# Token-tile tail, norm from PSUM, direct operand sums and waits by tile in a one-core hybrid layer

## The chip, the cores and the metric

The kernel runs on one core of a Trainium2 chip. The core has TensorE (PE) for matmuls, VectorE (DVE), ScalarE (ACT), GpSimd (POOL) and SyncE (SP, which here only issues transfers). The metric is the device time of one execution, in microseconds.

## What is computed

One decoder layer on `x` of 1 x 2048 x 1024 in fp32:

```python
h = rmsnorm(x, pre_mix_norm);  p = h @ w_in
mix = concat(pool_mixer(p), ssd_mixer(p), mlstm_mixer(p)) @ w_out
x = x + rmsnorm(mix, post_mix_norm)
h = rmsnorm(x, pre_ffn_norm)
u = causal_dwconv(h @ w_up, conv_w, conv_b)      # 2 x 2816 columns, 3 taps
g, val = split(u)
f = (gelu(g) * val) @ w_down
x = x + rmsnorm(f, post_ffn_norm)
```

## The kernel before

The 2048 tokens are four blocks `s` of 512 (`TB`), each of four token tiles of 128 (`NCK`). All matmuls are in pairs of a high and a low fp32r part: `mm3` (L124) does three matmuls of 128 x 128 by 128 x 512 for one fp32 product, so every operand passes a split: a cast on ACT for the high part, a subtraction on DVE for the low.

The four mixers run first, one block after the other, and store their output transposed in DRAM. Then, for each block: `load_mix` (L708) loads and splits it into two operand tiles of the T buffers; `out_proj` (L717) multiplies it with `w_out` in two halves of 512 columns, 96 matmuls each, with four token tiles in the four PSUM banks of `psm`, and copies each bank out on ACT; `mid_norm` (L726) does the first norm with the residual add (stored to DRAM as `x2_d`) and the second norm; `to_T` (L751) transposes the result on PE, 32 transposes of 128 x 128 per block, copies it out on ACT and stores it in `hT_d`.

The feed-forward layer works on two pairs of blocks. The up and the down matrix products are each done with seven products of half-sized operands in place of eight. `prep_T` (L773) builds their operand sums from `hT_d` and puts the split parts into T0 to T6; `prep_T_last` (L792) loads the last two. `up` (L849) takes 22 column tiles, each with 7 products of 12 matmuls, then the convolution and gelu on ACT, DVE and POOL. `down_first` (L965) does two of the down products (`product`, L933: eleven steps `kp` of 24 matmuls, eight PSUM banks, one per token tile), `down_rest` (L994) the other five, and `finish` (L978) the last norm and the residual add, token tile by token tile. `finish` is called for the second four tiles of a pair after the last product is complete. `up` of the first pair starts between `out_proj` of block 3 and `to_T` of block 3, which it calls after its first column tile (`after_first`, L1093).

The order on each engine is worked out before the run by a scheduler from the program's dependencies; two calls of `keep_in_program_order` (L730, L758) pin single instructions. Each engine then works through its own list in order, as SP's and POOL's queues do with transfers. Pools `bt` (T2 to T6), `bm` and `be` lie over memory that the mixers or `bt` used before, and a first use waits for the whole pool's earlier users. In the names below, `acc0` and `acc1` hold the rows of even and odd blocks, `psm` banks are `mm`, `pss` banks are `sm`.

Of the kernel before, what the change touches and what calls it, by code (L numbers as in the profile page):

```python
# [8 lines left out]
F32 = mybir.dt.float32  # L9
F32R = mybir.dt.float32r  # L10
# [5 lines left out]
P = 128  # L16
# [45 lines left out]
def kernel(  # L62
# [35 lines left out]
    for nm in ("post_mix", "pre_ffn"):  # L98
        nw[nm] = shared.tile([P, DM], F32, tag=nm, name=nm)
    junk = shared.tile([P, DM], BF16, name="junk")  # L100
# [7 lines left out]
    V.memset(mhalf, -0.5)  # L108

# [40 lines left out]
    with ExitStack() as actx:  # L150
# [18 lines left out]
        def load_x(s, ws=None):  # L169
# [41 lines left out]
            (pool_scale[0].rearrange("(t p) -> t p", p=P), 2),  # L211
        ]
# [11 lines left out]
        V.tensor_copy(out=vcol[:, 66:nrow], in_=pv[:, 66:nrow])  # L224
        pbs = ac.tile([P, 2], F32, name="pbs")
# [48 lines left out]
        for nm, src in (("post_mix", post_mix_norm), ("pre_ffn", pre_ffn_norm)):  # L274
            nc.gpsimd.dma_start(out=nw[nm], in_=src[0].partition_broadcast(P))
# [394 lines left out]
    with ExitStack() as bctx:  # L670
        bm = bctx.enter_context(tc.tile_pool(name="bm", bufs=1))
# [16 lines left out]
        bsh.adopt("cv", [a1[:, 3072:4096]])  # L688

# [13 lines left out]
        def rms_scale(t):  # L703
# [13 lines left out]
        def out_proj(mT):  # L717
            mo = [sh.tile([P, DM], F32, tag="acc", name="mo") for _ in range(NCK)]
            lhs = lambda kt: (mT[kt // 4][:, kt % 4, 0], mT[kt // 4][:, kt % 4, 1])
            for hf in range(2):  # L720
                ps = proj_tm(lhs, w_out, 0, KT, hf)
                for tok in range(NCK):
                    S.copy(out=mo[tok][:, hf * 512:(hf + 1) * 512], in_=ps[tok])
            return mo

        def mid_norm(s, mo):  # L726

            ss = sb.tile([P, 2 * NCK], F32, tag="ss4", name="ss4", bufs=1)[:, :NCK]
            for tok in range(NCK):
                i = S.activation(out=junk, in_=mo[tok], func=AF.Square, accum_out=ss[:, tok:tok + 1])  # L730
                if s == 1 and tok == 0:
                    tc.keep_in_program_order(i)
            rs1 = rstd_from(ss, DM, [P, NCK], sb, "n4", 1)
            prev = None
            for tok in range(NCK + 1):
                if tok < NCK:
                    t = mo[tok]
                    r = s * TB + tok * P
                    xt = sh.tile([P, DM], F32, tag="xt", name="xt")
                    nc.sync.dma_start(out=xt, in_=x2d[r:r + P])  # L740
                    V.scalar_tensor_tensor(out=t, in0=t, scalar=rs1[:, tok:tok + 1], in1=nw["post_mix"],
                                           op0=ALU.mult, op1=ALU.mult)
                    V.tensor_tensor(out=t, in0=t, in1=xt, op=ALU.add)
                    nc.sync.dma_start(out=x2_d[s][tok * P:(tok + 1) * P], in_=t)
                    rs = rms_scale(t)
                if prev:
                    V.scalar_tensor_tensor(out=prev[0], in0=prev[0], scalar=prev[1][:, 0:1], in1=nw["pre_ffn"],
                                           op0=ALU.mult, op1=ALU.mult)
                prev = (t, rs)
# [21 lines left out]
        TI = {"T2": 2, "B11": 3, "T1": 4, "T3": 0, "B21": 1, "T4": 5, "B22": 6}  # L771

        def prep_T(sb_, Tt):  # L773

            for kt in range(4):
                l1, l2 = Lm[:, 0:1024], Lm[:, 1024:2048]
                nc.sync.dma_start(out=l1, in_=hT_d[sb_][kt * P:(kt + 1) * P])
                nc.sync.dma_start(out=l2, in_=hT_d[sb_][(kt + 4) * P:(kt + 5) * P])
                a_, b_, c_, d_ = l1[:, :512], l1[:, 512:], l2[:, :512], l2[:, 512:]
                put = lambda n, x: split(x, Tt[TI[n]][:, kt, 0], Tt[TI[n]][:, kt, 1])  # L780
                put("B11", a_)
                V.tensor_tensor(out=a_, in0=b_, in1=a_, op=ALU.subtract)
                put("T1", a_)
                V.tensor_tensor(out=b_, in0=d_, in1=b_, op=ALU.subtract)
                put("T3", b_)
                put("B21", c_)
                V.tensor_tensor(out=a_, in0=d_, in1=a_, op=ALU.subtract)
                put("T2", a_)
                V.tensor_tensor(out=c_, in0=c_, in1=a_, op=ALU.subtract)
                nc.gpsimd.dma_start(out=T4_d[sb_][kt * P:(kt + 1) * P], in_=c_)  # L790

        def prep_T_last(sb_, Tt):  # L792
            for n, src in (("T4", T4_d[sb_]), ("B22", hT_d[sb_][512:1024, 512:1024])):
                t = Tt[TI[n]]
                nc.sync.dma_start(out=t[:, :, 1].bitcast(F32), in_=src.rearrange("(k p) l -> p k l", p=P))
                for h in range(2):
                    d = t[:, 2 * h:2 * h + 2]
                    S.copy(out=d[:, :, 0], in_=d[:, :, 1].bitcast(F32))
                    V.tensor_tensor(out=d[:, :, 1], in0=d[:, :, 1].bitcast(F32), in1=d[:, :, 0].bitcast(F32),  # L799
                                    op=ALU.subtract)  # L800
# [333 lines left out]
```

## Time and profile before

| what | us |
|---|---|
| runs (3), median | 2282.2 |
| lowest and highest run | 2279.72, 2283.53 |
| the profiled execution | 2281.67 |
| its span in the trace | 2280.0 |
| PE busy | 2163.8 |
| DVE busy | 1667.6 |
| ACT busy | 1008.4 |
| POOL busy | 540.0 |

Busy times are shares of one span and overlap. Matmuls are pipelined, so that a matmul's own record is longer than the distance to the next. A granted clock of 1.00 in a window is TensorE's full 2.4 GHz, and 0.50 is its lower level, 1.2 GHz.

### The profile page before, as it was taken

To read this page: it belongs to the slowest core of one execution; us is meant where nothing else is said; L and a number is where in the kernel's file an instruction comes from. 1 tells how busy PE (TensorE), PEld (TensorE's weight loads), DVE (VectorE), ACT (ScalarE), POOL (GpSimd) and SP (SyncE) were. 2 spreads that over 40 slices of the span, in tenths; PEclk is the share of its full clock that TensorE was granted. 3 is DMA by queue.
4 is the path that set the end of the run, shared out by engine and by line. 5 is a ranking of instruction groups with operands and counts; after the bars stand their busy time and mean duration, and the time that the engine had idled before them with its cause. 6 is when DMAs were issued, how large, how long until landed. Compare 5 with 4: busy or idle time off the path is not lost.

```text
span 2280.0 us, 27273 instructions
## 1 busy us (share of the span) xinstructions
PE 2163.8 (95%) x9773; PEld 1752.0 (77%) x9773; DVE 1667.6 (73%) x2374; ACT 1008.4 (44%) x1517; POOL 540.0 (24%) x779
## 2 busy tenths in 40 slices
PE   7999999999997996699999999999999999999994
PEld 5887887878886885478888887788888887788883
DVE  5888888888776576678888777447888788654854
ACT  4454364364353565354444444344444444322432
POOL 3222233222222123555555531000101010000101
PEclk9999999999998998799999999999999999999997
DMA  6444353352352777634444446555655556753753
GB/s 215 121 134 128 105 184 91 115 170 87 108 157 74 246 254 255 215 120 139 148 138 134 135 130 227 170 191 164 209 172 190 195 191 231 286 176 110 232 193 120
DMA packets 223785, 379.66 MB, mean 167 GB/s; under 512 B 15062, under 2 KB 122866, under 8 KB 223649
## 3 DMA queue, kind: packets, MB, share of 16 engines
q1 hardware_dynamic: 192352, 272.67, 37.5%
q0 software_dynamic: 28992, 96.86, 12.0%
q10 hardware_dynamic: 2304, 8.39, 1.1%
q8 instruction: 76, 1.25, 0.2%
q14 instruction: 61, 0.49, 0.1%
HBM read 274.48 MB, written 103.38 MB: 166 GB/s over the span
## 4 chain that ended last, share of the span: by engine, by line
PE 87%; DMA 5%; DVE 3%; ACT 2%; issue 2%; POOL 1%; SPq 0%; DVEq 0%; ACTq 0%; POOLq 0%
PE mm L126 18%; PE mm L127 18%; PE mm L128 18%; PE sm L126 8%; PE sm L128 8%; PE sm L127 8%; PE sm L490 1%; DMA wraw<-in_w_in_dram 1%; PE sm L537 1%; DMA Lm<-hT 1%; DMA T<-Lm 1%; DMA out_dram<-xt 1%; PE sm L493 1%; PE sm L500 1%; PE sm L542 1%
## 5 line engine op out<-in xcount | busy, mean ns | idle before, releaser
L126 PE MATMUL mm<-T,wsp 128*128 128x512 f32 x1152 | 459.7, 400 | 9.9 <-ACT T L182 4.1
L127 PE MATMUL mm<-T,wsp 128*128 128x512 f32 x1152 | 455.6, 396 | 0.0
L128 PE MATMUL mm<-T,wsp 128*128 128x512 f32 x1152 | 453.3, 397 | 0.0
L126 PE MATMUL mm<-wsp,T 128*128 128x512 f32 x748 | 297.6, 402 | 16.6 <-ACT wsp L768 8.5
L127 PE MATMUL mm<-wsp,T 128*128 128x512 f32 x748 | 295.7, 395 | 0.0
L128 PE MATMUL mm<-wsp,T 128*128 128x512 f32 x748 | 292.3, 394 | 0.0
L863 DVE SCALAR_TENSOR_TENSOR acc<-acc,fcol,acc 128x1024 f32<-128x1024 f32 x176 | 235.1, 1336 | 44.7 <-ACT acc L860 40.3
L126 PEld LDWEIGHTS mm<-T,wsp 128*128 128x128 f32 x1152 | 217.6, 189 | 60.5 <-issue 5.5
L127 PEld LDWEIGHTS mm<-T,wsp 128*128 128x128 f32 x1152 | 217.7, 189 | 48.9 <-issue 1.0
L128 PEld LDWEIGHTS mm<-T,wsp 128*128 128x128 f32 x1152 | 217.6, 189 | 49.0 <-issue 0.5
L126 PE MATMUL sm<-T,wsp 128*128 128x512 f32 x528 | 210.6, 399 | 8.7 <-ACT wsp L768 8.0
L128 PE MATMUL sm<-T,wsp 128*128 128x512 f32 x528 | 209.5, 398 | 2.7 <-DVE wsp L769 2.7
L127 PE MATMUL sm<-T,wsp 128*128 128x512 f32 x528 | 209.9, 397 | 0.9 <-DVE T L799 0.9
L118 DVE TENSOR_TENSOR wsp<-wraw,wsp 128x1024 fp32r<-128x1024 f32 x120 | 147.7, 1232 | 78.8 <-ACT wsp L117 78.3
L117 ACT CAST wsp<-wraw 128x1024 fp32r<-128x1024 f32 x120 | 125.9, 1050 | 158.1 <-PE mm L128 79.0
L126 PEld LDWEIGHTS mm<-wsp,T 128*128 128x128 f32 x748 | 141.7, 190 | 49.2 <-ACT wsp L768 9.0
L127 PEld LDWEIGHTS mm<-wsp,T 128*128 128x128 f32 x748 | 141.5, 189 | 30.5 <-issue 0.5
L128 PEld LDWEIGHTS mm<-wsp,T 128*128 128x128 f32 x748 | 140.7, 188 | 30.7 <-DVE T L715 0.2
L768 ACT CAST wsp<-xt 128x512 fp32r<-128x512 f32 (+1 forms) x98 | 80.6, 826 | 144.3 <-PE sm L127 94.8
L769 DVE TENSOR_TENSOR T<-T 128x1024 fp32r<-128x1024 f32 x59 | 72.1, 1223 | 91.6 <-ACT T L768 83.1
L860 ACT ACTIVATE acc<-acc,fcol 128x1024 f32<-128x1024 f32 x88 | 109.9, 1249 | 48.8 <-DVE acc L921 47.8
L768 ACT CAST T<-T 128x1024 fp32r<-128x1024 f32 x59 | 62.1, 1053 | 147.9 <-DMA T<-aop 138.1
(355 smaller groups left out, 3959.7 us busy)
## 6 DMA issues: line engine op xcount, KB each, us to landing
wraw<-in_w_in_dram SPq DMA_DIRECT2D x88, 512.0 KB, 3.7
T<-aop SPq DMA_DIRECT2D x59, 512.0 KB, 3.7
aop<-acc POOLq DMA_DIRECT2D x44, 512.0 KB, 3.1
upS<-Lm POOLq DMA_DIRECT2D x66, 256.0 KB, 3.4
wraw<-in_w_out_dram SPq DMA_DIRECT2D x32, 512.0 KB, 4.2
wraw<-in_ffn_w_down_dram SPq DMA_DIRECT2D x28, 512.0 KB, 4.3
xt<-upS SPq DMA_DIRECT2D x53, 256.0 KB, 4.1
xt<-in_ffn_w_up_dram SPq DMA_DIRECT2D x26, 512.0 KB, 4.5
```

Of the source, the lines that this page charges most:

```text
L117: S.copy(out=sp[:, 0], in_=raw)
L118: V.tensor_tensor(out=sp[:, 1], in0=raw, in1=sp.bitcast(F32)[:, 0], op=ALU.subtract)
L126: T.matmul(out=acc, lhsT=lw[0], rhs=lx[0], start=first, stop=False, skip_group_check=goes_on)
L127: T.matmul(out=acc, lhsT=lw[0], rhs=lx[1], start=False, stop=False, skip_group_check=goes_on)
L128: T.matmul(out=acc, lhsT=lw[1], rhs=lx[0], start=False, stop=last, skip_group_check=goes_on)
L490: T.matmul(out=py[:, h], lhsT=m[:, h], rhs=xd[:, h], start=True, stop=True)
L493: T.matmul(out=po[:, g * 4:g * 4 + 4], lhsT=ck(ccm[g], c), rhs=st[:, g * 4:g * 4 + 4], start=True, stop=True)
L500: T.matmul(out=pst[:, g * 4:g * 4 + 4], lhsT=bt[:, g], rhs=dx[:, g * 4:g * 4 + 4], start=True, stop=True)
L768: S.copy(out=hi, in_=src)
L769: V.tensor_tensor(out=lo, in0=src, in1=hi.bitcast(F32), op=ALU.subtract)
L860: S.activation(out=c, in_=u[:, 2:], func=AF.Identity, scale=fcol[:, 88 + t:89 + t], bias=fcol[:, 132 + t:133 + t])
L863: V.scalar_tensor_tensor(out=c, in0=u[:, k:k + 2 * TB], scalar=fcol[:, k * NU + t:k * NU + t + 1], in1=c, op0=ALU.mult, op1=ALU.add)
```

## The change

1. `product` gets `tail`: with `tail=6`, in the last product only, the steps `kp` 6 to 10 are held back and done token tile by token tile (15 matmuls each), and each token tile's `finish` follows at once. Residual rows are loaded into eight buffers during the product (five slices of `b12m`, three `xt`); the square sum and the `post_ffn` multiply of the right half are done ahead (`weigh`).
2. `out_proj` takes the square sums on ACT and the multiply with `post_mix` on DVE straight from PSUM. `mid_norm` then needs one multiply-add per token tile; the second norm's scale is an ACT copy, and `pre_ffn` is applied in the copy after the transposes (`preT`, one column per k tile). Transposes go by k tile over four token tiles (`turn`, `normed`).
3. Operand sums of the first pair take block 1 directly from the rows that the transposed copy leaves in SBUF; only block 0's half is loaded back from `hT_d`. `prep(0)` stands before `out_proj` of block 2. The T buffers are given out anew: block 1 uses T2 and T3, blocks 2 and 3 both T5 and T6.
4. Pools `bt`, `bm` and `be` wait by tile (`reuse_waits="tile"`); the pins are gone. `down_first` copies through eight buffers of 512 columns instead of whole rows; `spare` takes the place of the `pre_ffn` buffer.

```diff
+        bt = btx.enter_context(tc.tile_pool(name="bt", bufs=1, reuse_waits="tile"))
+        bm = bctx.enter_context(tc.tile_pool(name="bm", bufs=1, side="right", reuse_waits="tile"))
...
         def out_proj(mT):
...
                 for tok in range(NCK):
-                    S.copy(out=mo[tok][:, hf * 512:(hf + 1) * 512], in_=ps[tok])
-            return mo
+                    S.activation(out=junk, in_=ps[tok], func=AF.Square, accum_out=ss[:, hf, tok:tok + 1])
+                    V.tensor_tensor(out=mo[tok][:, c], in0=ps[tok], in1=nw["post_mix"][:, c], op=ALU.mult)
+            return mo, ss
...
+        def mid_norm(s, mo, ss):
+            V.tensor_tensor(out=ss[:, 0], in0=ss[:, 0], in1=ss[:, 1], op=ALU.add)
+            rs1 = rstd_from(ss[:, 0], DM, [P, NCK], sb, "n4", 1)
...
+                V.scalar_tensor_tensor(out=t, in0=t, scalar=rs1[:, tok:tok + 1], in1=xt,
+                                       op0=ALU.mult, op1=ALU.add)
+                nc.sync.dma_start(out=x2_d[s][tok * P:(tok + 1) * P], in_=t)
+                rs = rms_scale(t, xt)
+                S.activation(out=t, in_=t, func=AF.Copy, scale=rs[:, 0:1])
...
+        def turn(s, kt):
+            ps = pss.tile([P, NCK, P], F32, tag="sm", name="ps_tr")
             for tok in range(NCK):
...
+                T.transpose(out=ps[:, tok], in_=cols(s, kt)[:, tok], identity=ident)
+            return ps
...
+        def normed(s, kt):
+            d = cols(s, kt)
+            S.activation(out=d, in_=turn(s, kt), func=AF.Copy, scale=preT[:, kt:kt + 1])
+            c = (s % 2) * TB
+            nc.gpsimd.dma_start(out=r4(hT_d[s // 2][kt * P:(kt + 1) * P, c:c + TB]), in_=d)
+            return d
...
-        def prep_T(sb_, Tt):
+        def prep(sb_):
             for kt in range(4):
...
+                b11, b21 = load_h(sb_, 0, kt), load_h(sb_, 0, kt + 4)
+                if sb_ == 0:
+                    b12, b22 = normed(1, kt), normed(1, kt + 4)
...
-        def product(au, ai, wload, ps, new, also=None):
+        def product(au, ai, wload, ps, new, also=None, tail=NKP):
...
+                    if kp >= tail:
+                        late.append((kp, ua, w, i))
+                        continue
...
+            if late:
+                for t in range(NT):
+                    for kp, ua, w, i in late:
+                        mm(kp, t, ua, w, i)
+                    also(kp, t)
...
+        def finish(tile_, left, right, xt, ss):
+            square_sum(left, ss[:, 0:1])
             V.tensor_tensor(out=ss[:, 0:1], in0=ss[:, 0:1], in1=ss[:, 1:2], op=ALU.add)
+            V.tensor_tensor(out=left, in0=left, in1=nw["post_ffn"][:, h0], op=ALU.mult)
             rs = rstd_from(ss[:, 0:1], DM, [P, 1], sb, "n")
+            for c, t in ((h1, right), (h0, left)):
+                V.scalar_tensor_tensor(out=xt[:, c], in0=t, scalar=rs[:, 0:1], in1=xt[:, c],
+                                       op0=ALU.mult, op1=ALU.add)
...
-            product("au6", 6, w_T4, ps, False)
+            product("au6", 6, w_T4, ps, False, finish_last, 6)
...
+        mo0 = block(0, T_mem)
+        load_mix(1, Tt[2:4])
+        mid_norm(0, *mo0)
+        mo1 = out_proj(Tt[2:4])
+        load_mix(2, Tt[5:7])
+        for kt in range(4):
+            put("B11", kt, normed(0, kt))
+        for kt in range(4):
+            put("B21", kt, normed(0, kt + 4))
...
+        mid_norm(1, *mo1)
+        prep(0)
+        mo2 = out_proj(Tt[5:7])
+        load_mix(3, Tt[5:7])
+        mid_norm(2, *mo2)
+        to_T(2)
+        mo3 = out_proj(Tt[5:7])
+        prep_last(0)
+        mid_norm(3, *mo3)
```

The order on VectorE at the end of the last mixer, before (`bd`, `hn`, `h`, `den` are the mixer's, `mt` its output, `n4v` the norm's scale):

```order
L587 TENSOR_TENSOR mt_1_1639<-sm_274,vcol 128x256
L741 SCALAR_TENSOR_TENSOR acc_195<-acc_195,n4v_5723,post_mix 128x1024 x4
L574 RECIPROCAL den_1572<-den_1572 128x4
L562 SCALAR_TENSOR_TENSOR bd<-bd,ar_1855,sm_455 64x65 x2
L547 TENSOR_TENSOR hn_1557<-sm_274,ar_1855 128x260
L562 SCALAR_TENSOR_TENSOR bd<-bd,ar_1855,sm_455 64x65 x2
L577 TENSOR_TENSOR h_0_1576<-h_0_1576,den_1572 128x256
L548 TENSOR_TENSOR hn_1557<-hn_1557,sm_224 128x260
```

And with the change, from the same `mt` row on:

```order
L589 TENSOR_TENSOR mt_1_1641<-sm_276,vcol 128x256
L575 TENSOR_TENSOR den_1574<-den_1574,ar_1857 128x4
L576 RECIPROCAL den_1574<-den_1574 128x4
L579 TENSOR_TENSOR h_0_1578<-h_0_1578,den_1574 128x256
L580 TENSOR_TENSOR hn_1523<-h_0_1578 128x4x64
L549 TENSOR_TENSOR hn_1559<-sm_276,ar_1857 128x260
L582 TENSOR_REDUCE mss_1582<-hn_1523 128x4
L550 TENSOR_TENSOR hn_1559<-hn_1559,sm_225 128x260
```

The four rows of `mid_norm` of block 0 that stood ahead of the RECIPROCAL are gone from there. The order on TensorE after the last matmul of `out_proj` of block 3, before (`acc_195` holds block 2's rows, `acc_196` block 3's; `x4` counts equal neighbours):

```order
L758 MATMUL sm_363<-ident,acc_195 128x128 x4
L758 MATMUL sm_455<-ident,acc_195 128x128 x4
L126 MATMUL mm_367<-T_5465,wsp_230 128x512
L758 MATMUL sm_224<-ident,acc_195 128x128 x4
L127 MATMUL mm_367<-T_5465,wsp_230 128x512
L128 MATMUL mm_367<-T_5465,wsp_230 128x512
L758 MATMUL sm_224<-ident,acc_196 128x128 x8
L126 MATMUL mm_367<-T_5465,wsp_230 128x512
L127 MATMUL mm_367<-T_5465,wsp_230 128x512
```

And with the change, at block 3's first transposes:

```order
L129 MATMUL mm_368<-T_5462,wsp_248 128x512
L127 MATMUL mm_368<-T_5462,wsp_248 128x512
L128 MATMUL mm_368<-T_5462,wsp_248 128x512
L129 MATMUL mm_368<-T_5462,wsp_248 128x512
L757 MATMUL sm_457<-ident,acc_196 128x128
L757 MATMUL sm_225<-ident,acc_196 128x128
L127 MATMUL sm_276<-T_5465,wsp_231 128x512
L128 MATMUL sm_276<-T_5465,wsp_231 128x512
L129 MATMUL sm_276<-T_5465,wsp_231 128x512
```

Before, block 2's last transposes and block 3's first stand among the first nine matmuls of `up`; with the change 72 matmuls of `up` stand ahead of block 3's first transpose, and none of block 2's is left there. The end of VectorE's list, before (`nv` is the last norm's scale):

```order
L989 SCALAR_TENSOR_TENSOR acc_195<-acc_195,nv_5732,post_mix 128x512
L989 SCALAR_TENSOR_TENSOR acc_196<-acc_196,nv_5732,post_mix 128x512
L989 SCALAR_TENSOR_TENSOR acc_195<-acc_195,nv_5741,post_mix 128x512
L989 SCALAR_TENSOR_TENSOR acc_196<-acc_196,nv_5741,post_mix 128x512
L991 TENSOR_TENSOR xt_250<-acc_195,xt_250 128x512
L991 TENSOR_TENSOR xt_250<-acc_196,xt_250 128x512
L991 TENSOR_TENSOR xt_233<-acc_195,xt_233 128x512
L991 TENSOR_TENSOR xt_233<-acc_196,xt_233 128x512
L991 TENSOR_TENSOR xt_239<-acc_195,xt_239 128x512
L991 TENSOR_TENSOR xt_239<-acc_196,xt_239 128x512
```

And with the change (`ssf` holds square sums, `sm` the last PSUM bank of the product):

```order
L1024 TENSOR_TENSOR ssf<-ssf 128x1
L1025 TENSOR_TENSOR acc_195<-acc_195,post_mix 128x512
L133 TENSOR_SCALAR nv_5738<-ssf 128x1
L1109 TENSOR_TENSOR acc_195<-acc_195,sm_225 128x512
L1028 SCALAR_TENSOR_TENSOR xt_240<-acc_196,nv_5738,xt_240 128x512
L1028 SCALAR_TENSOR_TENSOR xt_240<-acc_195,nv_5738,xt_240 128x512
L1024 TENSOR_TENSOR ssf<-ssf 128x1
L1025 TENSOR_TENSOR acc_195<-acc_195,post_mix 128x512
L133 TENSOR_SCALAR nv_5747<-ssf 128x1
L1028 SCALAR_TENSOR_TENSOR xt_251<-acc_196,nv_5747,xt_251 128x512
L1028 SCALAR_TENSOR_TENSOR xt_251<-acc_195,nv_5747,xt_251 128x512
```

Before, the scale, multiply and add of several token tiles follow the product; with the change each token tile has its own short run, and no separate add is left.

## Rows read from the trace of the kernel before

**Rows 1.** The page: span, and busy time, share and instructions by engine.

```profile
span 2280.0 us, 27273 instructions
...
PE 2163.8 (95%) x9773; PEld 1752.0 (77%) x9773; DVE 1667.6 (73%) x2374; ACT 1008.4 (44%) x1517; POOL 540.0 (24%) x779
```

**Rows 2.** Windows: us, busy time by engine, granted clock, DMA share, GB/s.

```profile
900.00:1000.00 100.00, 66.94 (x265) 50.82 (x265) 64.89 (x69) 37.88 (x59) 51.78 (x61) 0.80 0.55 183
1100.00:1200.00 100.00, 100.00 (x432) 80.82 (x432) 79.64 (x89) 47.57 (x67) 52.16 (x69) 1.00 0.42 137
2200.00:2280.00 80.00, 47.44 (x207) 38.49 (x205) 36.08 (x64) 18.17 (x39) 6.39 (x8) 0.82 0.32 111
```

**Rows 3.** Windows, finer, the same columns.

```profile
721.00:745.00 24.00, 11.55 (x42) 9.12 (x42) 17.97 (x42) 3.32 (x4) 7.22 (x10) 0.51 0.19 54
840.00:884.00 44.00, 44.00 (x200) 35.56 (x199) 30.88 (x39) 22.32 (x38) 13.43 (x14) 1.00 0.79 275
884.00:938.00 54.00, 18.56 (x69) 12.46 (x68) 37.61 (x45) 26.89 (x49) 25.09 (x31) 0.61 0.74 246
938.00:1010.00 72.00, 63.49 (x265) 49.65 (x264) 45.07 (x47) 30.62 (x45) 37.07 (x46) 0.94 0.43 140
```

**Rows 4.** Timeline of TensorE: start, us, line, tiles, count, [idle before and releaser].

```profile
734.20 0.69 PE L585 MATMUL sm<-ident,h 128*128 128x128 f32 x2 [6.74 <-DVE h L582]
...
741.29 0.80 PE L126 MATMUL mm<-wsp,T 128*128 128x512 f32 x1 [4.33 <-ACT T L714]
...
890.80 1.14 PE L758 MATMUL sm<-ident,acc 128*128 128x128 f32 x8 [2.91 <-ACT acc L762]
914.64 1.09 PE L758 MATMUL sm<-ident,acc 128*128 128x128 f32 x4 [20.38 <-ACT junk L705]
...
934.78 0.79 PE L126 MATMUL sm<-T,wsp 128*128 128x512 f32 x1 [7.05 <-ACT wsp L768]
...
1943.18 1.22 PE L126 MATMUL mm<-wsp,T 128*128 128x512 f32 x2 [8.52 <-ACT wsp L768]
```

**Rows 5.** Timeline of TensorE: its last matmul.

```profile
2247.05 0.39 PE L128 MATMUL sm<-wsp,T 128*128 128x512 f32 x1
```

**Rows 6.** Chain that ended last, at its end: start us, us, what.

```profile
2259.01 4.28 DMA xt<-x
...
2264.83 0.15 DVE nv L132
2264.99 5.20 DMA out_dram<-xt
...
2270.20 4.33 DMA xt<-x
...
2274.62 0.69 DVE xt L991
```

**Rows 7.** Groups of instructions after 2247 us: busy us, mean ns, idle before.

```profile
L989 DVE SCALAR_TENSOR_TENSOR acc<-acc,nv,post_mix 128x512 f32<-128x512 f32 x16 | 11.2, 745 | 1.2 <-POOL nv L133 1.2
...
L985 ACT ACTIVATE junk<-acc 128x512 bf16<-128x512 f32 x12 | 7.6, 632 | 5.9 <-DVE ss L986 4.5 <-DVE nv L132 1.0
L133 POOL TENSOR_TENSOR nv<-nv,mhalf 128x1 f32<-128x1 f32 x7 | 5.8, 847 | 13.2 <-DVE ss L986 11.1 <-DVE nv L132 2.1
L985 ACT ACTIVATION_READ_ACCUMULATOR junk<-acc 128x1 f32 x12 | 2.3, 188 | 0.0
L1051 DVE TENSOR_TENSOR acc<-acc,sm 128x512 f32<-128x512 f32 x2 | 1.4, 680 | 0.0
```

**Rows 8.** Timeline of VectorE, end of the last mixer.

```profile
724.01 4.86 DVE L741 SCALAR_TENSOR_TENSOR acc<-acc,n4v,post_mix 128x1024 f32<-128x1024 f32 x4
```

**Rows 9.** Chain that ended last, at the turn to down_rest.

```profile
1938.38 2.48 DVE acc L863 x2
1940.86 1.15 DVE t1m L1007
1942.08 1.06 ACT wsp L768
```

More of the change, by code (lines that the diff above doesn't have):

```diff
@@ L97 @@
     nw = {}
-    for nm in ("post_mix", "pre_ffn"):
-        nw[nm] = shared.tile([P, DM], F32, tag=nm, name=nm)
-    junk = shared.tile([P, DM], BF16, name="junk")
+    nw["post_mix"] = shared.tile([P, DM], F32, name="post_mix")
+    spare = shared.tile([P, DM], F32, name="spare")
+    junk = shared.tile([P, 512], BF16, name="junk")
     sh.adopt("acc", [m[:, i * DM:(i + 1) * DM] for m in acc_mem for i in range(4)])
@@ L272 @@
                 V.memset(icnt[r:r + 64, g // 2, t:t + 1], 1.0 / (t + 1))
[L274 to L275 removed]
+        nc.gpsimd.dma_start(out=nw["post_mix"], in_=post_mix_norm[0].partition_broadcast(P))
         st = ac.tile([P, 8, 64], F32, name="st")
@@ L721, in out_proj @@
                 ps = proj_tm(lhs, w_out, 0, KT, hf)
+                c = slice(hf * 512, (hf + 1) * 512)
                 for tok in range(NCK):
-                    S.copy(out=mo[tok][:, hf * 512:(hf + 1) * 512], in_=ps[tok])
-            return mo
-        def mid_norm(s, mo):
-            ss = sb.tile([P, 2 * NCK], F32, tag="ss4", name="ss4", bufs=1)[:, :NCK]
-            for tok in range(NCK):
[L730 to L749, printed above, removed]
@@ L767, in split, with to_T @@
+        def to_T(s):
+            for kt in range(KT):
+                normed(s, kt)
         def split(src, hi, lo):
@@ L792, in prep_T_last @@
-        def prep_T_last(sb_, Tt):
-            for n, src in (("T4", T4_d[sb_]), ("B22", hT_d[sb_][512:1024, 512:1024])):
-                t = Tt[TI[n]]
[L795 to L800, printed above, removed]
+        TI = {"T2": 0, "B11": 1, "T1": 2, "T3": 3, "B21": 4, "T4": 5, "B22": 6}
@@ L931, with mm @@
         NT = 2 * NCK
-        def product(au, ai, wload, ps, new, also=None):
+        def product(au, ai, wload, ps, new, also=None, tail=NKP):
+            def mm(kp, t, ua, w, i):
+                ts_ = slice(t * P, (t + 1) * P)
+                mm3(ps[t], (ua[:, 0, ts_], ua[:, 1, ts_]), (w[:, 0, i], w[:, 1, i]),
+                    new and kp == 0, kp == NKP - 1, not new)
+            late = []
             for u in range((NKP + 1) // 2):
@@ L965, in down_first @@
         def down_first(between):
-            N = [sh.tile([P, DM], F32, tag="acc", name="n11") for _ in range(NT)]
             ps = banks()
@@ L970, in down_first @@
             for t in range(NT):
-                S.copy(out=N[t][:, h0], in_=ps[t])
+                o = bsh.tile([P, 512], F32, tag="st", name="st")
+                S.copy(out=o, in_=ps[t])
+                nc.sync.dma_start(out=c1_d[t][:, h0], in_=o)
             between()
@@ L1024, in w_T4, with weigh, load_e1 @@
                 return diff(r_, r_, t1(u, n))
-            for t in range(NT):
-                nc.sync.dma_start(out=c21[t], in_=c1_d[t][:, h0])
+            ss = bm.tile([P, 2 * NT, 2], F32, name="ssf")
+            def weigh(tile_, right):
+                square_sum(right, ss[:, tile_, 1:2])
+                V.tensor_tensor(out=right, in0=right, in1=nw["post_ffn"][:, h1], op=ALU.mult)
+            def load_e1(kp):
+                if kp < NT:
+                    nc.sync.dma_start(out=c21[kp], in_=c1_d[kp][:, h0])
             ps = banks()
-            product("au6", 2, w_T1, ps, True)
+            product("au6", 2, w_T1, ps, True, load_e1)
             for t in range(NT):
```

154 lines of the change are left out of this document (76 added, 78 removed).

## The prediction

> **What bounds it now.** The page's busy table comes first: TensorE is busy 2163.8 of 2280.0 us [rows 1], and only what it loses in gaps or at half clock can be won. The windows by 100 us say where: a full window has 432 matmul records, one per 0.2325 us to the finer spacing of the timeline, but 900 to 1000 has 265 at clock 0.80, and the last 80 us have 47.44 us of work [rows 2]. Finer windows show that 884 to 938 holds 69 PE records in 54 us at clock 0.61, while 840 to 884 is full, 44.00 us at clock 1.00, with the DMA engines busy 0.79; 721 to 745 runs at 0.51 [rows 3]. PE's timeline names what it waited for: 6.74 us for the mixer's `h` on DVE, 4.33 for the first operand cast of block 1, 20.38 for the square of mid_norm(3) on ACT ahead of block 3's first transpose, 7.05 for an up weight, 8.52 at the turn to the last products [rows 4]. So the limit is TensorE, except in three places where short chains over ACT, DVE and POOL have no matmuls beside them: 721 to 745, 884 to 1010, and the end. PE's last matmul starts at 2247.05 [rows 5], ending near 2247.4, 32.6 us before the span ends.
>
> The sum is made against the profiled execution, 2281.67 us (1.7 more than its span); the median of the runs is 2282.2, so the same difference gives 0.5 us more there. Measurements of this kernel can tell about 0.2%, 4.6 us.
>
> **Part 1, the stretch from out_proj(1) to the first up products.** From 884 to 1010 us TensorE executed 69 + 265 = 334 instructions [rows 3]: 64 transposes (blocks 2 and 3) and 270 up matmuls. Without gaps and at full clock, 270 x 0.2325 = 62.8 and 64 x 0.14 (eight in 1.14 us [rows 4]) = 9.0, 71.8 of 126 us: 54.2 lost. The order of the change puts block 2's transposes among out_proj(3)'s matmuls and block 3's behind 72 up matmuls instead of 9, so 72 x 0.2325 = 16.7 us cover mid_norm(3). That does not hide it all. The bare chain of mid_norm(3) is: last bank square 0.63 + 0.19 and multiply 0.68, sum and scale 0.15 each, power 0.85 [rows 6, 7]; four multiply-adds of 1024, 4.9 by the four L741 [rows 8]; for the last token tile a square (twice the 0.63), 0.15, 0.85, and a scaled copy, costed like the square: together 11 us. Transposes by column need all four token tiles, so this whole chain counts. About ten casts and splits of weights and operands stand between its links on ACT and DVE, at 0.6 to 0.7 us each for those of 512; that makes about 18 to 22 us, against 16.7. I take a wait of 3 and as much again for half clock behind it: 6 us. For out_proj(2) and (3) I take 3 more: blocks 2 and 3 now use the same T5 and T6, whose casts wait for out_proj(2) to let go of each; and banks are held longer. **Bounds** for all that stays: 2 us (only the overlap's ends) and 22 (the old 20.38 in a new place, partly covered). Taken: 9, nearer to the small end, since row 840 to 884 shows the same two engines keeping up beside full PE.
>
> Bank evacuation: an ACT copy becomes square (0.82) then DVE multiply (0.68) [rows 7], 1.5 us. Block halves use the same four banks; between a bank's last matmul of one half and its first of the next lie 3 x 6 matmuls, 4.2 us. Cover 2.7 us: price nothing, as long as DVE's queue is not later than that. What is removed: mid_norm's separate adds and multiplies by pre_ffn (off PE's path except above) and half of prep(0)'s loads, 8 of 256 KB on SP instead of 8 of 512 KB. The transposed stores stay 32 on POOL's queue. T4 and B22 come by eight loads of 256 KB on SP in place of two of 1 MB, ahead of up weights. These beside the shorter loads I cost at nothing; their cover is out_proj(3), and gone it would be one landing, inside the 22.
>
> The mixer's end: T2's casts no longer wait for the whole pool, so the 4.33 goes. The four L741, 4.86 us ahead of the mixer's last RECIPROCAL on DVE [rows 8], now stand behind its last output; in their place four PSUM multiplies (4 x 0.68 = 2.7) come earlier, while PE still has work. Gain between 4.86 - 2.7 = 2.1 and 4.86, taken 3.0; late next is the mixer's own chain. Part 1: 54.2 + 4.3 + 3.0 - 9 = **52.5 saved**.
>
> **Part 2, the end.** Before, residual rows and stores of eight token tiles go through three `xt` buffers: store, load (4.28), add, store (5.20), load (4.33), add, in turn [rows 6]. The change loads all eight rows during the product (on SP, ahead of later weight loads), weighs the right half in advance, and does the last five of the product's eleven k steps token tile by token tile: 15 matmuls each, 3.49 us, against DVE's 0.68 + 0.68 + 2 x 0.75 + 2 x 0.15 = 3.2 [rows 6, 7]. DVE keeps up. After the last matmul: add 0.68; two multiply-adds of the tile before, 1.49 (the last square, 0.82, lies beside them); 0.15; multiply 0.68; 0.15; power 0.85; two multiply-adds 1.49: 5.5, with handoffs 5.8. Store and program end: the last add of before ends near 2274.62 + 1.29 (as a pair takes) = 2275.9, 4.1 before the end. Sum 9.9 instead of 32.6: **22.7 saved**; bounds 20 (a store of 5.20 and a late scale) to 24.3.
>
> **Part 3, the turn to down_rest.** Its chain is two conv steps (2.48), the first weight difference (1.15), its cast (1.06) [rows 9]; waits by tile let the b12m load start some matmuls earlier, but in DVE's new order three conv steps still precede the difference, on the last up bank. Saved 1; bounds 4 and -3. The turn to down_first keeps its order: 0.
>
> **Part 4, the start.** `spare`'s first load of 512 KB now stands seventh on SP's queue, amid the first input loads: at 275 GB/s [rows 3] it holds the engines 1.9 us. Bounds 0 and 1.9; taken 1 lost. Sum: 2281.7 - 52.5 - 22.7 - 1 + 1 = **2206**. With every bound at its end it is 2194 or 2227.
>
> **Rivals.** *The wait moves, not goes* (0.13): column transposes wait for four token tiles, the chain is late by its old 20.38, and an up weight behind it on ACT by its 7.05 [rows 4]. For it: each engine works its rows in the written order, and DVE was busy 37.61 of 54 us in 884 to 938 [rows 3]. Against: 63 more matmuls stand ahead. 2206 + 27 = 2233.
>
> *PE loses its clock in the out projections* (0.03, slower). Place: the halves of out_proj(1) to (3). If DVE's multiply of a bank is over 2.7 us late half after half, PE waits a little at each group, and as in 721 to 745 the granted clock is 0.51, the 1.2 GHz level [rows 3]. 576 matmuls at 0.465 instead of 0.2325 cost 134: 2340. It is slower than before once more than 75 / 0.2325 = 323 matmuls run so. Against: 840 to 884 cycles the same banks at 1.00. The Trainium skill has such a case (TensorE: Matmul & The Clock Gate, A second HAM failure mode: psum-queue depth-cycling): matmul groups going round PSUM banks with short idle moments between them made the clock swing. By that rule the time is this rival's 2340; the trace disagrees so far, with 1.00 in that window, and no run yet shows the two-engine evacuation.
>
> *The change does not do what it says in one part* (0.02): tile waits that still cover whole pools, or DVE so late that the end stays long: parts 2 and 1 each lose most. About 2282, no change.
>
> **Chances.** Forecast 0.82, of which its own bounds are 2194 to 2227; rivals 0.13, 0.03, 0.02. Range 2192 to 2236, to take in the first rival. Faster by over 0.2%: 0.82 + 0.13 less a hundredth for an unseen mishap, 0.94; within 0.2%: 0.02; slower 0.04.
>
> **What would show it.** Right: first transpose of block 3 after some 72 up matmuls, with a gap of a few us instead of 20.38; clock near 1 in the 100 us after out_proj(3); no 4.33 wait at out_proj(1); the L1028 multiply-adds last on DVE and under 11 us from last matmul to end; the 8.52 still 7 or more. Wrong: a gap above 10 us in front of a transpose or of T5's cast, clock 0.5 inside out_proj, PE waiting between token tiles at the end, or up weights landing late behind prep loads.

## The result, and the profile after

The changed kernel takes 2206.9 us (median of 4 runs, 2202.3 to 2209.2) against 2282.9: the ratio is 0.9666, with a 95% interval of 0.9647 to 0.9686. The forecast was 2206, so the total was met almost exactly; the parts were not, as the runs below show. The profiled execution took 2209.2 us, with a span of 2207.5, which is 72.5 less than the span before. The medians are 75.9 apart. Of the 3.4 us more, 2.3 come from that execution being the slowest of its four, and the rest from the profiled execution of before lying 1.2 under its median. Below, times of the runs are set against 2207.2 us, the mean of the two medians of the changed kernel (this one, and 2207.5 when it ran once more as e11).

The top of the page and finer windows of the changed kernel, the latter answering to [rows 3]:

```profile
span 2207.5 us, 27392 instructions
...
PE 2159.4 (98%) x9773; PEld 1749.0 (79%) x9773; DVE 1662.2 (75%) x2387; ACT 1011.8 (46%) x1541; POOL 547.7 (25%) x779
```

```profile
840.00:884.00 44.00, 44.00 (x207) 35.85 (x206) 26.33 (x38) 26.70 (x45) 9.98 (x13) 1.00 0.78 269
884.00:938.00 54.00, 45.81 (x194) 34.72 (x194) 36.56 (x42) 31.17 (x54) 34.90 (x43) 0.94 0.77 246
938.00:1010.00 72.00, 70.19 (x301) 55.98 (x300) 62.82 (x66) 35.48 (x50) 43.53 (x53) 1.00 0.44 144
```

The window 884 to 938 now holds 194 instructions instead of 69, at clock 0.94 instead of 0.61. Window 840 to 884 stays full at 1.00, with banks now emptied by ACT and DVE one after the other. TensorE's timeline has what is left of the waits of [rows 4]:

```profile
729.70 0.69 PE L587 MATMUL sm<-ident,h 128*128 128x128 f32 x2 [3.34 <-DVE h L584]
733.51 0.69 PE L587 MATMUL sm<-ident,h 128*128 128x128 f32 x2 [3.12 <-DVE h L584]
...
837.33 0.50 PE L127 MATMUL mm<-wsp,T 128*128 128x512 f32 x1 [2.32 <-DVE acc L731]
...
889.70 0.50 PE L127 MATMUL mm<-T,wsp 128*128 128x512 f32 x1 [1.62 <-DVE acc L731]
908.29 0.50 PE L127 MATMUL sm<-T,wsp 128*128 128x512 f32 x1 [1.60 <-DVE acc L936]
913.92 0.66 PE L757 MATMUL sm<-ident,acc 128*128 128x128 f32 x4 [1.24 <-ACT acc L747]
916.10 0.79 PE L127 MATMUL mm<-T,wsp 128*128 128x512 f32 x1 [1.53 <-ACT wsp L776]
...
1893.99 2.08 PE L127 MATMUL mm<-wsp,T 128*128 128x512 f32 x4 [6.70 <-ACT wsp L776]
```

No wait is over 2.4 us between 740 and 1010; the wait for block 3's norm is 1.24 where it was 20.38, and 4.33 at the start of out_proj(1) is gone. Two of block 3's transposes stand behind 72 up matmuls, as forecast; 14 follow behind 84 and 16 behind 96. At the end, TensorE's last matmul and VectorE's last rows:

```profile
2198.33 0.40 PE L129 MATMUL sm<-wsp,T 128*128 128x512 f32 x1
```

```profile
2198.77 0.69 DVE L1109 TENSOR_TENSOR acc<-acc,sm 128x512 f32<-128x512 f32 x1 [0.74 <-PE sm L129]
2199.37 1.41 DVE L1028 SCALAR_TENSOR_TENSOR xt<-acc,nv,xt 128x512 f32<-128x512 f32 x2
2200.70 0.15 DVE L1024 TENSOR_TENSOR ssf<-ssf 128x1 f32<-128x1 f32 x1
2200.77 0.68 DVE L1025 TENSOR_TENSOR acc<-acc,post_mix 128x512 f32<-128x512 f32 x1
2201.37 0.14 DVE L133 TENSOR_SCALAR nv<-ssf 128x1 f32<-128x1 f32 x1
2202.18 1.41 DVE L1028 SCALAR_TENSOR_TENSOR xt<-acc,nv,xt 128x512 f32<-128x512 f32 x2 [0.66 <-POOL nv L134]
```

VectorE waits 0.74 for each token tile's last matmul, so it keeps up; 8.8 us lie between the last matmul's end and the end of the span, 32.6 before.

**Where the 72.5 us came from.** All kernels here execute the same 8424 `mm3` matmuls, so the start of the n-th one can be compared between traces. Times of stretches in us, each the difference of two such starts (the last row: end of the span less the last start and 0.4):

| matmuls | what | before | after | after, again |
|---|---|---|---|---|
| 0 to 500 | start, first mixer | 151.2 | 147.4 | 147.5 |
| 500 to 2200 | mixers | 525.2 | 525.4 | 527.4 |
| 2200 to 2304 | end of the last mixer | 57.0 | 53.1 | 52.3 |
| 2304 to 3150 | the middle: out_proj(1) to the first 270 up matmuls | 269.2 | 233.7 | 233.2 |
| 3150 to 4710 | rest of the first up | 361.8 | 361.9 | 361.9 |
| 4710 to 5000 | turn to down_first | 73.5 | 68.7 | 69.9 |
| 5000 to 7000 | second up | 464.2 | 464.3 | 464.4 |
| 7000 to 7110 | turn to down_rest | 35.9 | 34.2 | 34.3 |
| 7110 to 8423 | last five products | 301.2 | 301.6 | 302.4 |
| end | after the last matmul | 32.6 | 8.8 | 8.8 |

The end gives 23.8, the middle 35.5, the mixer's end 3.9, the start 3.8, the two turns 6.5; the other rows are 0.1 to 0.4 longer.

### The profile page after: what moved, and what is told of

Its sections match the earlier page's. It is cut to its first block, busy times and chain, and to the rows that moved or that the text cites. A ratio compares the mean times of both kernels' runs of the same rounds, so it can differ in the third digit from the quotient of the medians.

```text
span 2207.5 us, 27392 instructions
## 1 busy us (share of the span) xinstructions
PE 2159.4 (98%) x9773; PEld 1749.0 (79%) x9773; DVE 1662.2 (75%) x2387; ACT 1011.8 (46%) x1541; POOL 547.7 (25%) x779
## 3 DMA queue, kind: packets, MB, share of 16 engines
q10 hardware_dynamic: 2304, 8.39, 1.2%
## 4 chain that ended last, share of the span: by engine, by line
PE 89%; DMA 3%; DVE 3%; issue 2%; ACT 1%; POOL 1%; SPq 0%; DVEq 0%; POOLq 0%; ACTq 0%
PE mm L127 19%; PE mm L129 19%; PE mm L128 19%; PE sm L127 8%; PE sm L128 8%; PE sm L129 8%; PE sm L539 1%; PE sm L492 1%; DMA wraw<-in_w_in_dram 1%; PE sm L544 1%; PE sm L502 1%; DMA xt<-mixT 1%; PE sm L495 1%; DMA T<-aop 0%; PE sm L547 0%
## 5 line engine op out<-in xcount | busy, mean ns | idle before, releaser
L777 DVE TENSOR_TENSOR T<-T 128x1024 fp32r<-128x1024 f32 (+1 forms) x75 | 84.6, 1132 | 97.6 <-ACT T L776 97.3
L875 POOL COPY acc<-fhalo 128x2 f32<-128x2 f32 x88 | 43.6, 496 | 410.0 <-DVE acc L882 330.2
L776 ACT CAST T<-T 128x1024 fp32r<-128x1024 f32 (+1 forms) x75 | 71.7, 960 | 145.2 <-DMA T<-aop 129.5
```

The costliest lines, as they stand in the source:

```text
L776: S.copy(out=hi, in_=src)
L777: V.tensor_tensor(out=lo, in0=src, in1=hi.bitcast(F32), op=ALU.subtract)
L875: G.tensor_copy(out=u[:, 0:2], in_=fhalo[:, t])
```

## The experiments

Labels e1 to e12; each time is a median of 4 runs or more, and the ratios with their intervals are to the kernel before.

**e1: the kernel before, with all of block 3's transposes pinned.** This edit alone:

```diff
-                        if s == 3 and tok == hf == j == 0:
+                        if s == 3:
```

> The kernel before, with one edit: all 32 transposes of block 3 are pinned behind everything that stands ahead of them in the program on TensorE, so that some 87 up matmuls (20 us) come first instead of 9. Nothing else of the change. Theory 1 (the big gap was a matter of cover: where the transposes stand): the 20.38 us wait and the 2.75 behind it vanish, the wait for an up weight stays at about 7, and the time falls by 20 to 30 us, to 2253 to 2263. Theory 2 (the chain of mid_norm(3) itself, with its separate multiplies and adds, is what was too long, so work from PSUM is what helps): the wait only moves behind the up matmuls or to the up weights, and less than 10 us is gained, 2273 to 2283.

2280.6 us, ratio 0.9991 (0.9982 to 1.0001): no gain. Its timeline of TensorE:

```profile
893.89 1.60 PE L758 MATMUL sm<-ident,acc 128*128 128x128 f32 x8 [2.92 <-ACT acc L762]
923.57 0.80 PE L126 MATMUL mm<-T,wsp 128*128 128x512 f32 x1 [25.95 <-ACT T L768]
...
937.29 0.80 PE L126 MATMUL sm<-T,wsp 128*128 128x512 f32 x1 [5.61 <-ACT wsp L768]
```

The wait for block 3's norm is gone (its first transpose stands behind 96 up matmuls in this trace), and 25.95 us stand in its place, for the cast of an operand tile T: an up operand that prep_T(0) had not finished. So the 20.38 of [rows 4] was only the first in TensorE's list of two chains that ended close together. The second can be seen in the chain of waits of the kernel before, where prep_T(0) goes through one buffer, `Lm`, and DRAM:

```profile
909.57 6.80 DMA T<-Lm
916.39 8.27 DMA Lm<-hT
```

A buffer is stored, 6.80, and only then loaded again, 8.27, for the next of four steps. Its loads ran from 852 to 925 us, after out_proj(2). Neither theory named this chain; of the two, the second's time holds.

**e2: the kernel before, with the new end alone.** The edit is part 1 of the change in `product`, `finish`, `finish_first` and `finish_last`; the square sums lie in a spent buffer.

```diff
...
-            product("au6", 6, w_T4, ps, False)
-            for t in range(NT):
-                V.tensor_tensor(out=c21[t], in0=c21[t], in1=ps[t], op=ALU.add)
-                finish(NT + t, c21[t], c22[t])
+            product("au6", 6, w_T4, ps, False, finish_last, 6)
```

> The kernel before, with part 1 of the change alone (last five steps token tile by token tile, residual rows ahead, right half weighed ahead). Theory: the end is worth what it was worth in the whole change, 32.6 us from last matmul to the end of the span become about 9, nothing before the last product moves, and the time falls by 23 to 24 us, to 2258 to 2260. Rival: the row loads ahead of the last weights delay the product, as the pools here wait for everything, and less than 18 is left.

2259.0 us, ratio 0.9891 (0.9876 to 0.9905): 24.5 less. The end is 9.8 us long where it was 32.6, and the stretches ahead of it are within 1.5 us of the kernel before. The end stands by itself.

**e3: the changed kernel, with the last product whole.**

```diff
-            product("au6", 6, w_T4, ps, False, finish_last, 6)
+            product("au6", 6, w_T4, ps, False, finish_last)
+            for t in range(NT):
+                finish_last(None, t)
```

> The changed kernel, but the last product whole again and all eight finishes behind it; rows are still loaded and right halves still weighed ahead. Theory (VectorE's eight times 3.2 us need matmuls beside them): the end takes 8 x 3.2 + 6 = 31 us instead of 8.8, the time is 2226 to 2230. Rival (the serial loads and stores through three buffers were the cost, and they are gone here too): the end takes 12 to 18 us, 2210 to 2216.

2220.7 us, ratio 0.9721 (0.9704 to 0.9737), between the two. The end takes 22.5 us. TensorE's last matmul, and VectorE's first and last rows behind the product:

```profile
2195.69 0.39 PE L129 MATMUL sm<-wsp,T 128*128 128x512 f32 x1
```

```profile
2191.36 2.05 DVE L1109 TENSOR_TENSOR acc<-acc,mm 128x512 f32<-128x512 f32 x3 [22.37 <-PE mm L129]
...
2211.97 2.74 DVE L1028 SCALAR_TENSOR_TENSOR xt<-acc,nv,xt 128x512 f32<-128x512 f32 x4 [0.54 <-POOL nv L134]
```

The theory had left out that in a whole product a bank's last matmul falls inside the last step's 24, so the first finishes already run beside 4.9 us of matmuls (7 x 3 x 0.2325): 8 x 3.1 - 4.9 + 3.9 for the last store gives 23.8, near it. Of the 23.8 us that the whole change gains at the end, 13.7 come from the order by token tile, and 10 from the rest of part 1: rows loaded and right halves weighed ahead, with one multiply-add in place of a multiply and an add. These were not tried apart.

**e4: the changed kernel, with block 3's transposes pinned.** In the trace the first of them stands behind 96 up matmuls in place of 72, not behind 108.

```diff
-                T.transpose(out=ps[:, tok], in_=cols(s, kt)[:, tok], identity=ident)
+                i = T.transpose(out=ps[:, tok], in_=cols(s, kt)[:, tok], identity=ident)
+                if s == 3:
+                    tc.keep_in_program_order(i)
```

> The changed kernel, with block 3's transposes pinned behind all that stands ahead in the program (108 up matmuls in place of 72). Theory (the 13 us that are still lost between 887 and 968 come mostly from block 3's norm being late for its transposes): 3 to 6 us are gained, 2201 to 2204. Rival (they come from weights and bank evacuations that share ACT and DVE with the norm, each late by 1 to 2 us): no gain, 2205 to 2210, the waits stand in other places.

2209.6 us, ratio 0.9675 (0.9661 to 0.9689): no gain, as the rival said. The 1.24 for the norm goes; the waits for an up weight are 2.52 and 2.14 now:

```profile
912.70 0.49 PE L127 MATMUL mm<-T,wsp 128*128 128x512 f32 x1 [2.52 <-ACT wsp L778]
```

**e5: the changed kernel, with pools waiting as a whole**; the same edit for `bm` and `be`:

```diff
-        bt = btx.enter_context(tc.tile_pool(name="bt", bufs=1, reuse_waits="tile"))
+        bt = btx.enter_context(tc.tile_pool(name="bt", bufs=1))
```

> The changed kernel with the three pools bt, bm and be waiting as a whole again, all else kept. Theory: the cast of the first operand of block 1 waits for the mixer's end again, 4 us before out_proj(1), and the first difference after the last up product comes 1 to 2 us later; 2211 to 2214. Rival (tile waits carry the gain of the middle too, because Lm, T5 and T6 can be filled earlier): the loss between 740 and 1010 grows by more than 15 us, 2225 or more.

2216.5 us, ratio 0.9701 (0.9688 to 0.9715), some 9 us more and past the theory's 2214. Two places answer, in TensorE's timeline:

```profile
740.24 0.80 PE L127 MATMUL mm<-wsp,T 128*128 128x512 f32 x1 [4.37 <-ACT T L718]
...
1902.99 2.08 PE L127 MATMUL mm<-wsp,T 128*128 128x512 f32 x4 [8.29 <-ACT wsp L776]
```

The wait of 4.33 at out_proj(1) is back, as 4.37, and the turn to down_rest is at 8.29 again, 1.6 more; the mixer's end is 4.7 us longer (57.8) and the turn 2.4 (36.6). The middle takes 232.3 us, no more than 233.7: the rival is out. The rest, 2.2 in the mixers and 1.7 at the turn to down_first, is of the size that such stretches vary by.

**e6: the changed kernel, with block 1's half loaded back from DRAM.**

```diff
-                if sb_ == 0:
-                    b12, b22 = normed(1, kt), normed(1, kt + 4)
-                else:
-                    b12, b22 = load_h(sb_, 1, kt), load_h(sb_, 1, kt + 4)
+                b12, b22 = load_h(sb_, 1, kt), load_h(sb_, 1, kt + 4)
+                if sb_ == 1:
...
+        to_T(1)
```

> The changed kernel, but prep(0) loads block 1's half back from DRAM too (transposes by to_T(1), eight more loads of 256 KB). Theory: prep(0) has out_proj(2) and (3) as cover, 46 us each, so the way through DRAM is hidden: 2205 to 2210. Rival (the direct sums are what brings prep(0) in on time): the first up matmuls wait for T buffers, 10 to 20 us lost, 2217 to 2227.

2212.8 us, ratio 0.969 (0.9677 to 0.9703), 5.5 more and outside the theory's numbers. But its middle takes 232.4 us, as long as with direct sums; what is longer is the mixers' stretch (529.3), where every engine's list is the same as in the changed kernel. No cost of the way through DRAM shows in this trace. The median's 5.5 us stay open: all four executions took 2211.9 to 2213.6, the changed kernel's eight 2202.3 to 2212.0, and only one of the four was traced.

**e7: the changed kernel, with banks copied out on ACT and the norm from SBUF.**

```diff
-                    S.activation(out=junk, in_=ps[tok], func=AF.Square, accum_out=ss[:, hf, tok:tok + 1])
-                    V.tensor_tensor(out=mo[tok][:, c], in0=ps[tok], in1=nw["post_mix"][:, c], op=ALU.mult)
+                    S.copy(out=mo[tok][:, c], in_=ps[tok])
...
+                V.scalar_tensor_tensor(out=t, in0=t, scalar=rs1[:, tok:tok + 1], in1=nw["post_mix"],
+                                       op0=ALU.mult, op1=ALU.mult)
+                V.tensor_tensor(out=t, in0=t, in1=xt, op=ALU.add)
```

> The changed kernel, but out_proj copies its banks out on ACT and mid_norm does squares, the multiply with post_mix and a separate add from SBUF, as before. Theory (the chain of mid_norm(3), now 11 us bare, grows by 4 x 1.2 for the adds and by 4 x 2 x 0.8 for squares that came beside matmuls): block 3's transposes wait 8 to 12 us longer, 2215 to 2222. Rival (72 matmuls of cover and freer banks make up for it, the two waits for L731 of 2.3 and 1.6 go): 2204 to 2210.

2224.4 us, ratio 0.9739 (0.9726 to 0.9753): 17 more, past the theory's end. Its timeline of TensorE:

```profile
733.65 0.69 PE L587 MATMUL sm<-ident,h 128*128 128x128 f32 x2 [7.97 <-DVE h L584]
...
914.14 0.80 PE L127 MATMUL sm<-T,wsp 128*128 128x512 f32 x1 [4.66 <-DVE acc L940]
921.18 0.55 PE L761 MATMUL sm<-ident,acc 128*128 128x128 f32 x3 [2.17 <-ACT acc L751]
924.62 1.12 PE L761 MATMUL sm<-ident,acc 128*128 128x128 f32 x4 [2.22 <-ACT acc L751]
927.46 1.12 PE L761 MATMUL sm<-ident,acc 128*128 128x128 f32 x4 [1.72 <-ACT acc L751]
```

The multiplies of 1024 stand ahead of the mixer's last rows again, and the wait for `h` is 7.97 instead of 3.34; the norm of block 3 is late for each transpose. The middle takes 243.5 us, 9.8 more. Norm from PSUM is the one part whose loss alone lengthens the middle by more than it varies (226.4 to 233.7 with the changed kernel's lists).

**e8: the changed kernel, with spare's first load kept from the start.**

```diff
         G.memset(fhalo, 0.0)
+        G.tensor_copy(out=spare[:, 0:1], in_=fcol[:, 0:1])
```

> The changed kernel, with one column of spare written from fcol after the mixers, so that its first load can't stand at the start. Theory (that load costs the input loads 1.9 us): 500 matmuls are done 0 to 2 us earlier than in the changed kernel, 2205 to 2207. Rival (the order of the start, in which this load is one piece, is what gained 3.7 us there): the wait of 4 us for the gate weights comes back, 2209 to 2212.

2209.0 us, ratio 0.9678 (0.9665 to 0.9691); 500 matmuls are done 0.8 us earlier. The total says nothing. The stretch, 146.3 us, agrees with the theory: the early load costs about a microsecond, no more than the same stretch varies with the changed kernel's lists (146.5 to 148.8 in after and e3 to e6). The wait for the gate weights does not come back, so the rival is out.

**e9: the changed kernel, with the T plan of before.**

```diff
-        TI = {"T2": 0, "B11": 1, "T1": 2, "T3": 3, "B21": 4, "T4": 5, "B22": 6}
+        TI = {"T2": 2, "B11": 3, "T1": 4, "T3": 0, "B21": 1, "T4": 5, "B22": 6}
...
-        prep(0)
-        mo2 = out_proj(Tt[5:7])
+        mo2 = out_proj(T_mem)
         load_mix(3, Tt[5:7])
         mid_norm(2, *mo2)
...
+        prep(0)
         mo3 = out_proj(Tt[5:7])
...
```

The plan brings two things with it: block 0's rows are split inside prep(0), and block 2's transposes are called behind out_proj(3). They were not tried apart.

> The changed kernel with the T buffers given out as before (block 1 in T5 and T6, block 2 in T0 and T1, so that two of the five operand tiles of the first pair can be filled only after out_proj(2)) and prep(0) behind out_proj(2); norm from PSUM, direct sums of block 1, tile waits and the new end are kept. Theory (from the run with pinned transposes: the big gap of before was the chain of prep(0) through one buffer and DRAM, which began too late): the wait for a T operand comes back with 15 to 30 us between 887 and 942, 2222 to 2237. Rival (with direct sums and double-buffered loads prep(0) is quick enough wherever it stands): within 5 us of the changed kernel, 2204 to 2212.

2227.6 us, ratio 0.9753 (0.9737 to 0.977): the theory's time, but not its place, so the time agrees by luck. TensorE never waits for a T operand; it waits inside out_proj(3), for a bank that VectorE empties late:

```profile
879.41 0.79 PE L127 MATMUL mm<-wsp,T 128*128 128x512 f32 x1 [10.77 <-DVE acc L731]
```

```profile
872.65 2.49 DVE L777 TENSOR_TENSOR T<-Lm,T 128x512 fp32r<-128x512 f32 x4
875.06 0.69 DVE L806 TENSOR_TENSOR Lm<-acc,Lm 128x512 f32<-128x512 f32 x1
875.66 1.29 DVE L777 TENSOR_TENSOR T<-acc,T 128x512 fp32r<-128x512 f32 x2
876.86 0.68 DVE L806 TENSOR_TENSOR Lm<-acc,Lm 128x512 f32<-128x512 f32 x1
877.47 0.69 DVE L808 TENSOR_TENSOR Lm<-Lm 128x512 f32<-128x512 f32 x1
878.07 0.68 DVE L777 TENSOR_TENSOR T<-Lm,T 128x512 fp32r<-128x512 f32 x1
878.67 2.48 DVE L731 TENSOR_TENSOR acc<-mm,post_mix 128x512 f32<-128x512 f32 x4
```

The four bank multiplies stand behind prep(0)'s splits and sums. The granted clock over the same stretch:

```profile
868.00:890.00 22.00, 11.23 (x40) 8.70 (x40) 14.28 (x23) 7.82 (x14) 5.99 (x10) 0.64 0.53 165
890.00:910.00 20.00, 20.00 (x88) 16.07 (x87) 14.97 (x21) 12.01 (x24) 7.69 (x9) 1.00 0.63 192
```

```profile
863.00:866.70 3.70, 1.54 (x13) 0.99 (x11) 1.23 (x1) 3.67 (x9) 0.94 (x2) 1.00 0.90 341
866.70:870.10 3.40, 1.94 (x9) 1.53 (x8) 2.37 (x4) 3.40 (x7) 3.09 (x5) 0.50 0.84 234
```

It stands at 0.50 from 866.70 us on, some 2 us before that wait begins at 868.64. Ahead of its fall TensorE had done transposes from 861.06, with waits of 0.39 and 2.16. So the long wait is not shown to be what lowered it.

Of the 15.6 us between the two spans, the whole middle has only 3.9 (237.6). Another 5.4 are at the mixer's end, where the transposes of the convolution weights wait for their load ahead of out_proj(1), a matter of where that list puts them; the turn to down_rest has 3.2.

```profile
740.71 0.41 PE L1130 MATMUL sm<-ident,Lm 88*128 88x88 f32 x1 [5.46 <-DMA Lm<-in_ffn_conv_w_dram]
```

**e10: the changed kernel, with the broadcast of pre_ffn put back at the start.**

```diff
+        nc.gpsimd.dma_start(out=spare, in_=pre_ffn_norm[0].partition_broadcast(P))
```

> The changed kernel with the broadcast of pre_ffn to 128 partitions put back at the start (into spare, where nothing reads it), which also keeps spare's first weight load away from there. Theory (this broadcast, 512 KB amid the first input loads, is what cost before its wait of 4 us at the gate weights): 500 matmuls are done 3 to 4 us later than in the changed kernel, 2210 to 2212. Rival (the start's gain came from another order of loads): no more than 1 us later, 2205 to 2209.

2208.1 us, ratio 0.9667 (0.9652 to 0.9681). The stretch follows the theory: 500 matmuls take 151.7 us, 4.3 more than in the changed kernel and as long as before, and the wait at the gate weights is back:

```profile
30.48 0.63 PE L360 MATMUL mm<-T,wg 128*32 128x512 f32 x1 [3.92 <-DVE wg L259]
```

The total follows the rival. In the profiled execution the middle was short, 227.5 us; the other three were not traced, so that these 4 us lengthen the whole is not shown.

**e11: the changed kernel once more.**

> The changed kernel itself once more. It shows how far the stretches vary from one run to the next, with which the single parts undone are compared: expected 2205 to 2209, and every stretch within 1.5 us of the first profile.

2207.5 us, ratio 0.9664 (0.9643 to 0.9685). Its stretches stand in the table above: all but the mixers' (2.0 apart) are within the 1.5 expected. Over all runs the middle varies more than that: e3 and e5 have the changed kernel's lists there, and took 226.4 and 232.3 us. In e3 the waits of 0.45 us or more between 740 and 1010 sum to 5.8 us, in the first profile to 13.6.

**e12: the T plan of before and the copies of e7 together**, the two diffs above in one kernel.

> The T plan of before as in the run before, and out_proj's banks copied out on ACT with the norm from SBUF as well; direct sums, tile waits, transposes by column and the new end are kept. Theory (with prep(0) late, the chain itself costs TensorE its 20 us, wherever the banks are emptied): the two losses add, 17 for the copies and 20 for the plan, 2240 to 2248, with the gap at the first up products instead of inside out_proj(3). Rival (the plan's 20 us came only from the bank multiplies that stand behind prep(0)'s work in VectorE's order): 2222 to 2230, as with the copies alone.

2243.6 us, ratio 0.9829 (0.9813 to 0.9845): the totals add (2207.2 + 17.2 + 20.4 = 2244.8), as the theory has it, and the rival is out. But the gap is again in another place than the theory said, at block 2's transposes inside out_proj(3):

```profile
872.34 1.12 PE L761 MATMUL sm<-ident,acc 128*128 128x128 f32 x4 [9.84 <-ACT acc L751]
```

The middle takes 254.2 us, 20.5 more than after, where the two parts alone cost 9.8 and 3.9; the 6.8 beyond their sum is within the 7.3 that the middle varies by. Another 8.0 us are at the mixer's end (61.1), with the wait for the convolution weights as in e9. So the total does not show that the chain of prep(0) costs TensorE 20 us.

## Why the prediction was right, and where not

**The sum.** Predicted 52.5 + 22.7 + 1 - 1 = 75.2 saved; measured 72.5 between the spans, 75.9 between the medians. Errors of both signs met: part 1 was 13.1 too high, the start 4.8 and the turn to down_first 4.8 too low, the turn to down_rest 0.7 and the end 1.1 too low. That the total came out to a microsecond is luck; the two large gains were where it put them. Its terms sum to 2206.5, and with the bounds that it gives for the mixer's end the outer times are 2192 and 2228, not 2194 and 2227.

**Part 1, the mis-sized term.** "Taken: 9" for all waits that stay. The middle saved 35.5 where 54.2 - 9 = 45.2 were forecast, so 18.7 stay. Thirteen us are waits of 0.5 to 2.4 us between 740 and 960, with clock 0.94 in 884 to 938: inside the bounds of 2 and 22, but at the far end. In e3, with the same lists, the middle saved 42.8, so that 9 was short by 2 to 10 us, depending on the execution. The waits are not the one late chain that was costed (1.24 for the norm, where 3 was forecast). Weight casts (1.53), the bank multiplies that were priced at nothing (2.32 and 1.62), and the sums that empty the banks of `up` (1.60) share ACT and DVE with the norm, and each comes 1 to 2 us late. e4 shows that moving the transposes does not remove them.

**Its reading of the gap.** The prediction took 20.38 for mid_norm(3) and paid for it with cover of 72 matmuls. e1 gives the kernel before about that cover, and it gains nothing, since prep_T(0) was late by as much. In the changed kernel the norm's wait is 1.24 us and none for an operand of prep(0) is left, so the forecast came through for a reason that it saw only half: prep(0)'s shorter loads it costed at nothing. No single part carries the middle. Without norm from PSUM 9.8 us come back and without both that and the T plan 20.5. Without the T plan alone it is 4, and without direct sums or tile waits nothing; none of these three can be told from the variation. What of the other 15 belongs to transposes by column, to prep(0)'s loads through four small buffers, or to several parts at once, was not tried apart.

**The mixer's end.** 7.3 forecast, 3.9 measured. The 4.33 went with tile waits (e5), and the multiplies did stand in the way (7.97 in e7 against 3.34), but of the gain in that gap the mixer's own chain gave back part: a second wait of 3.12 on `h`, 1.39 long before in its place. The two waits on `h` together shrank from 8.13 to 6.46, by 1.7 where 3.0 was taken. With the 4.33 that makes 6.0; why 3.9 were measured (4.8 in e11) stays open.

**The end, the turns, the start.** 9.9 forecast for the end and 8.8 measured; its split into rows ahead and order by tile was not forecast. The turn to down_rest was right in its mechanism, three conv steps still ahead of the difference, and 1.7 against 1 saved; its wait is 6.70, just under the sign "still 7 or more". The start failed: `spare`'s load cost about the microsecond taken (e8), but the prediction passed over a removed transfer of the same size, the broadcast of `pre_ffn`, which was worth 4 there (e10). The turn to down_first was called unmoved and gave 4.8; e1, without the change, already takes 2.7 less there than the kernel before, so up to about half may be variation, and the rest stays open.

**The rivals.** A moved gap did not come. The loss of clock in out_proj did not come in the changed kernel (1.00 from 740 to 840 and in 840 to 884). The case of the Trainium skill named there (TensorE: Matmul & The Clock Gate, A second HAM failure mode: psum-queue depth-cycling) was not put to the test by it: it has short idle moments between the groups, and here TensorE is busy for all 44.00 us of the window 840 to 884 and waits for a bank once before it (2.32). The prediction's "the trace disagrees so far" rests on the window of before, which is as full. What e9 shows is another thing, one wait of 10.77 us for a bank whose multiply stands behind other work on DVE. With it the middle is 3.9 us longer than after, and 11.2 longer than the shortest with the changed kernel's lists, not 134. The price in that 134 was too high as well: at clock 0.50 the matmuls of the kernel before start 0.43 us apart (937.07, 937.50, 937.93), not 0.465.

## What to carry to other kernels

A wait in the trace names what ended last, not what would have ended next: before a gap is put down to one chain, look in the list of the waiting engine for the next instruction, and when its own operands were ready. Best is to try the cheap reordering by itself, as in e1. At a product's end, loading residuals and weighing ahead (10 us here) and finishing output tile by output tile (13.7) were both worth having, and e2 shows that together they need nothing else of the change. Giving the emptying of a PSUM bank to an engine with other work makes each thing ahead of it in that engine's list a possible stall of TensorE.

## What the runs showed that was not expected

A broadcast of one row of 4 KB to 128 partitions, issued on POOL while the first inputs load, put 4 us onto the start (500 matmuls in 150.9 to 151.7 us with it, 146.3 to 148.8 without it). And the same lists of instructions took 226.4 to 233.7 us in the middle stretch in four executions (after, e11, e3, e5): what shifts from one execution to the next was not traced to a cause, but it moves the stretch by 3%, so parts under 7 us there can't be ranked by one profile each.
